# The mLSTM's maximum and weight rows: spread by matmuls with the identity instead of through DRAM

## The chip, the cores and the metric

One core of one Trainium2 chip runs the whole program. The metric is the device time of one execution in microseconds (us). Several runs are taken, and their median is given.

## The reference, cut to what matters

Two transformer blocks are computed in f32 over 1024 tokens of width 1024. The first has gated linear attention and a feed-forward part. The second has a token mixer with two halves side by side, an mLSTM with 4 heads and a latent attention with 8 heads, and then a second feed-forward part. Only the mLSTM is touched. Its recurrence over the tokens t, for each head, is

```
m_t = max(log f_t + m_{t-1}, i_t)
C_t = exp(log f_t + m_{t-1} - m_t) C_{t-1} + exp(i_t - m_t) v_t k_t^T      (n_t in the same way, with k_t alone)
h_t = C_t q_t / max(|n_t . q_t|, exp(-m_t))
```

It is computed by chunks: inside a chunk by a masked product of queries and keys, weighted by exp(D - m) with D the sums of the log gates, and across chunks by the state C. The weights need the running maximum m as a value for each query (the columns of the scores as they lie here) and for each key (the rows).

## The kernel before, in words

The kernel is one function, `tile_blocks`, with its work written out stage after stage. Matmuls of the projections take their operands split into a high and a low part and issue three products for each (L117 to L119, helper `mm3`); the mLSTM's own matmuls are plain f32.

The mLSTM works on 8 chunks of 128 tokens. A row loop (L1184 to L1203) first makes, for each chunk, four rows per head in a tile `rw` with the heads on 4 partitions: the key's value (row 0), the maximum plus the sum of gates (row 1), the exponent of the state's weight (row 2), and the key's exponent for the state (row 3). The running maximum itself is a separate tile `M_`, made by a scan on VectorE. Four transposes on TensorE (`pc`, L1202) turn the rows into columns, 16 numbers for each token, which VectorE copies to `cols`.

The chunk function `ml_chunk` needs the maximum and row 2 the other way round: the 128 queries along the free dimension and the same row on every partition. Before the change the row loop writes `M_` and row 2 to a DRAM tile `m_scr` (L1198, L1199), and each chunk reads them back with a source that repeats (L1359 for `mb`, 256 KB on arrival; two at L1363 for `wb`, 64 KB each). Then:

- ScalarE takes the exponential of `wb` (L1364). VectorE subtracts the key's column from `mb` for each of 4 heads (L1366), ScalarE takes the exponential (L1367), GpSimd applies the causal mask (L1368).
- TensorE makes the scores `msc` (L1375), VectorE multiplies them into `mb` (L1376). GpSimd scales the queries by `wb` (L1379, `mqw`). TensorE makes numerators and denominators `mnu` from `mb` (L1386) and from the state (L1388).
- TensorE transposes the keys (`mkp`, L1394), ScalarE scales them (`mkw`, L1397), TensorE makes the chunk's part of the state (`mkv`, L1402), VectorE adds it to the old state times `wb`'s last column (`mC`, L1408). The statistics `mst` and the scaled output `hn` follow (L1415 to L1428).

`mb` and `wb` have two buffers each. `msc`, `mkp` and `mkv` share two banks of PSUM (tag `y`); `mnu`, and before it `pg` and `pc`, share two (tag `tr`). Four banks (tag `big`) serve the fillers.

The fillers are projections of the attention half: 32 units with 8 matmul triples or fewer each into `pst`, then what is done with them (a norm with `cq`, a gate `to`), the transposes `pcn` of the latents and the values `pv`. Before each chunk some of them are issued (`per_chunk`), by a generator.

What each engine does in which order is fixed when the program is built: a planner goes by the order of the text and its own estimates of times, and the chunks come with a priority that is 400 instructions ahead:

```
    per_chunk = [8, 8, 6, 3, 2, 2, 2, 2]
    ...
    for t in range(NT):
        for _ in range(per_chunk[t]):
            next(units, None)
        with tc.high_priority(offset=ML_AHEAD):
            C_ = ml_chunk(t, C_)
```

All transfers are issued from SyncE's one queue, in order, and an instruction there that waits holds up those behind it.

Of the kernel before, what the change touches and what calls it, by code (L numbers as in the profile page):

```python
# [10 lines left out]
F32 = mybir.dt.float32  # L11
# [3 lines left out]
AF = mybir.ActivationFunctionType  # L15
ALU = mybir.AluOpType
# [4 lines left out]
P = 128  # L21
S = 1024
D = 1024
NT = S // P
# [15 lines left out]
def tile_blocks(ctx, tc, A, out):  # L40
    nc = tc.nc
    act, dve, pool, pe, dma = nc.scalar, nc.vector, nc.gpsimd, nc.tensor, nc.sync
# [6 lines left out]
    def nm(base):  # L49
        uid[0] += 1  # L50
        return f"{base}{uid[0]}"
# [8 lines left out]
    dram = ctx.enter_context(tc.tile_pool(name="dram", bufs=1, space=DRAM))  # L60
# [24 lines left out]
    def psum_big(n):  # L85
        return psb.tile([P, 512], F32, tag="big", name=nm(n), bufs=4)

    ident = const.tile([P, P], F32, name="ident")
# [115 lines left out]
    o_scr = dram.tile([S, 512], F32, name="o_scr")  # L204
    h_scr = dram.tile([S, 512], F32, name="h_scr")
    r_scr = dram.tile([4, 2, S], F32, name="r_scr")
    m_scr = dram.tile([4, 2, S], F32, name="m_scr")
    x1_scr = dram.tile([S, D], F32, name="x1_scr")

    f_scr = dram.tile([7, (FF // 256 - 2) * P, HALF], F32, name="f_scr")  # L210
# [64 lines left out]
    for t in range(NT):  # L275
# [9 lines left out]
        if t % 4 == 3:  # L285

            hf = t // 4
            c = slice(hf * HALF, (hf + 1) * HALF)
# [10 lines left out]
    for h0 in range(0, GH, 2):  # L299
# [3 lines left out]
        for i, (h, d) in enumerate(items):  # L303
            e, a = e4[:, i], a4[:, i]
            for hf in range(2):
                c = slice(hf * HALF, (hf + 1) * HALF)
# [6 lines left out]
        for i, (h, d) in enumerate(items):  # L313
            e, a = e4[:, i], a4[:, i]
# [204 lines left out]
    for h in range(GH):  # L519
# [3 lines left out]
        for _ in range(PANELS[h]):  # L523
            i = next(n_panels)
# [100 lines left out]
    for j in range(8):  # L625
# [5 lines left out]
        for hf in range(2):  # L631
            c = slice(hf * HALF, (hf + 1) * HALF)
# [492 lines left out]
    vpl = open_pool(ml, "vpl", side="right")  # L1125
    c2 = open_pool(ml, "c2", side="right")
    cv = ExitStack()
    cp = open_pool(cv, "cp", side="right")
# [50 lines left out]
    pool.memset(ro[:, 1, :], 0.0)  # L1179
    m0 = vpl.tile([4, 1], F32, name="m0")  # L1180
    pool.memset(m0, 0.0)
    cols = vpl.tile([P, NT, 16], F32, name="cols")
    mprev = m0
    for t in range(NT):  # L1184
        pt = ps2.tile([P, 512], F32, tag="tr", name=nm("pg"))
        pe.transpose(pt[0:4, 0:P], gts[:, t, 0:4], ident)
        pe.transpose(pt[0:4, P:2 * P], logf[:, t, :], ident)
        b_ = cp.tile([4, P], F32, tag="rb", name=nm("rb"), bufs=2)
        rw = cp.tile([4, 4, P], F32, tag="rw", name=nm("rw"), bufs=3)
        M_ = cp.tile([4, P], F32, tag="rM", name=nm("rM"), bufs=2)  # L1190
        dve.tensor_tensor_scan(out=b_, data0=ro[:, 0, :], data1=pt[0:4, P:2 * P], initial=0.0, op0=ALU.mult, op1=ALU.add)
        dve.tensor_sub(out=rw[:, 0, :], in0=pt[0:4, 0:P], in1=b_)
        dve.tensor_tensor_scan(out=M_, data0=ro[:, 1, :], data1=rw[:, 0, :], initial=mprev, op0=ALU.add, op1=ALU.max)
        dve.tensor_add(out=rw[:, 1, :], in0=b_, in1=M_)
        dve.tensor_scalar(out=rw[:, 2, :], in0=M_, scalar1=-1.0, scalar2=mprev, op0=ALU.mult, op1=ALU.add)
        dve.tensor_scalar(out=rw[:, 3, :], in0=rw[:, 0, :], scalar1=M_[:, P - 1:P], scalar2=None, op0=ALU.subtract)
        mprev = rw[:, 1, P - 1:P]
        dma.dma_start(out=m_scr[:, 0, t * P:(t + 1) * P], in_=M_)  # L1198
        dma.dma_start(out=m_scr[:, 1, t * P:(t + 1) * P], in_=rw[:, 2, :])  # L1199
        pc = ps2.tile([P, 512], F32, tag="tr", name=nm("pc"))  # L1200
        for i in range(4):
            pe.transpose(pc[:, 4 * i:4 * i + 4], rw[:, i, :], ident[0:4, 0:4])  # L1202
        dve.tensor_copy(out=cols[:, t, :], in_=pc[:, 0:16])  # L1203

    act.activation(out=cols[:, :, 4:8], in_=cols[:, :, 4:8], func=AF.Exp, scale=-1.0)
    act.activation(out=cols[:, :, 12:16], in_=cols[:, :, 12:16], func=AF.Exp)
# [148 lines left out]
    def ml_chunk(t, C_):  # L1355
        c = slice(t * P, (t + 1) * P)

        mb = mla.tile([P, 4, P], F32, tag="mb", name=nm("mb"), bufs=2)
        dma.dma_start(out=mb, in_=m_scr[:, 0, c].unsqueeze(0).broadcast_to([P, 4, P]))  # L1359
        wb = mla.tile([P, 2, P], F32, tag="wb", name=nm("wb"), bufs=2)  # L1360
        mw = m_scr.rearrange("(a b) q s -> b q a s", b=2)
        for b2 in range(2):
            dma.dma_start(out=wb[64 * b2:64 * b2 + 64], in_=mw[b2, 1, :, c].unsqueeze(0).broadcast_to([64, 2, P]))  # L1363
        act.activation(out=wb, in_=wb, func=AF.Exp)  # L1364
        for h in range(4):
            dve.tensor_scalar(out=mb[:, h, :], in0=mb[:, h, :], scalar1=cols[:, t, h:h + 1], scalar2=0.0, op0=ALU.subtract, op1=ALU.max)  # L1366
        act.activation(out=mb, in_=mb, func=AF.Exp, scale=-1.0)  # L1367
        pool.tensor_mul(out=mb, in0=mb, in1=selm.unsqueeze(1).broadcast_to([P, 4, P]))  # L1368

        mb4 = mb.rearrange("p (a b) s -> p a b s", b=2)  # L1370
        for b2 in range(2):
            sc = psum_y("msc")
            r = slice(64 * b2, 64 * b2 + 64)
            for j in range(2):
                pe.matmul(sc[:, j * P:(j + 1) * P], mk[r, j, c], mq[r, j, c], start=True, stop=True)  # L1375
            dve.tensor_mul(out=mb4[:, :, b2, :], in0=sc[:, 0:256].rearrange("p (h s) -> p h s", h=2), in1=mb4[:, :, b2, :])  # L1376
        if C_ is not None:
            qw = mlp_.tile([P, 2, P], F32, tag="qw", name=nm("mqw"), bufs=2)
            pool.tensor_mul(out=qw, in0=mq[:, :, c], in1=wb)  # L1379
        nums = []  # L1380
        for h2_ in range(2):
            nu = ps2.tile([P, 512], F32, tag="tr", name=nm("mnu"), bufs=2)
            for p2 in range(2):
                r = slice(64 * h2_, 64 * h2_ + 64)
                o = nu[:, p2 * 130:p2 * 130 + 130]
                pe.matmul(o, mb4[:, p2, h2_, :], va[t][:, 2 * p2 + h2_], start=True, stop=C_ is None)  # L1386
                if C_ is not None:
                    pe.matmul(o, qw[r, p2], C_[r, p2], start=False, stop=True)  # L1388
            nums.append(nu)

        if t < NT - 1:
            kp = psum_y("mkp")
            for p2 in range(2):
                pe.transpose(kp[:, p2 * P:(p2 + 1) * P], mk[:, p2, c], ident)  # L1394
            kw = mla.tile([P, 4, 64], F32, tag="kw", name=nm("mkw"), bufs=2)
            for h in range(4):
                act.activation(out=kw[:, h], in_=kp[:, h * 64:(h + 1) * 64], func=AF.Copy, scale=cols[:, t, 12 + h:13 + h])  # L1397
            Cn = mla.tile([P, 2, 130], F32, tag="C", name=nm("mC"), bufs=2)
            for p2 in range(2):
                kv = psum_y("mkv")  # L1400
                h0 = 2 * p2
                pe.matmul(kv[:, 0:260], kw[:, h0:h0 + 2].rearrange("p a b -> p (a b)"), va[t][:, h0:h0 + 2].rearrange("p a b -> p (a b)"), start=True, stop=True)  # L1402
                for h2_ in range(2):
                    r = slice(64 * h2_, 64 * h2_ + 64)
                    if C_ is None:
                        act.copy(out=Cn[r, p2], in_=kv[r, h2_ * 130:h2_ * 130 + 130])
                    else:
                        dve.scalar_tensor_tensor(out=Cn[r, p2], in0=C_[r, p2], scalar=wb[r, p2, P - 1:P], in1=kv[r, h2_ * 130:h2_ * 130 + 130], op0=ALU.mult, op1=ALU.add)  # L1408
            C_ = Cn

        st = mlp_.tile([P, 16], F32, tag="mst", name=nm("mst"), bufs=2)
        jk = mlp_.tile([P, P], BF16, tag="mj", name=nm("mj"), bufs=1)
        for b2 in range(2):
            n3 = nums[b2][:, 0:260].rearrange("p (h e) -> p h e", h=2)
            act.activation(out=st[:, b2:b2 + 3:2], in_=n3[:, :, 128], func=AF.Abs)  # L1415
            for a2 in range(2):
                act.activation(out=jk, in_=n3[:, a2, 0:128], func=AF.Square, accum_out=st[:, 4 + 2 * a2 + b2:5 + 2 * a2 + b2])
        dve.tensor_max(st[:, 0:4], st[:, 0:4], cols[:, t, 4:8])
        dve.reciprocal(out=st[:, 0:4], in_=st[:, 0:4])
        dve.tensor_mul(out=st[:, 8:12], in0=st[:, 0:4], in1=st[:, 0:4])  # L1420
        dve.tensor_mul(out=st[:, 8:12], in0=st[:, 8:12], in1=st[:, 4:8])
        rstd_of(st[:, 8:12], 128, 4, st[:, 12:16], st[:, 4:8])
        dve.tensor_mul(out=st[:, 8:12], in0=st[:, 12:16], in1=st[:, 0:4])
        hn = mlp_.tile([P, 512], F32, tag="hn", name=nm("hn"), bufs=1)
        for h in range(4):
            dve.scalar_tensor_tensor(out=hn[:, h * P:(h + 1) * P], in0=nums[h % 2][:, (h // 2) * 130:(h // 2) * 130 + 128],
                                     scalar=st[:, 8 + h:9 + h], in1=hnb[:, h * P:(h + 1) * P], op0=ALU.mult, op1=ALU.mult)
        dma.dma_start(out=h_scr[t * P:(t + 1) * P, :], in_=hn)  # L1428
        return C_
# [186 lines left out]
    for i in range(len(rows) + DC + 1):  # L1616
        if i < len(rows):
            h, t = rows[i]
# [11 lines left out]
        if 0 < i <= len(rows):  # L1630
            h, t = rows[i - 1]
            if h % 2 == 1 and t in ((3, 7) if h == 7 else (7,)):
                att_recip(h // 2, t - 3 if h == 7 else 0, 4 if h == 7 else 8)
        if 0 <= i - DB < len(rows):
            h, t = rows[i - DB]
# [122 lines left out]
```

## Time and profile before

| | us |
|---|---|
| runs | 2745.82, 2746.67, 2744.04; median 2745.82 |
| the profiled execution's own time | 2743.75 |
| its span in the trace | 2742.0 |
| TensorE busy (matmuls) | 2622.4 (96%) |
| VectorE busy | 1770.7 (65%) |
| ScalarE busy | 1138.5 (42%) |
| GpSimd busy | 787.5 (29%) |
| mean granted clock of TensorE | 0.979 |

In the trace PE is TensorE, PEld its loads of weights, DVE VectorE, ACT ScalarE, POOL GpSimd and SP SyncE; a "q" behind the name is that engine's sequencer or its queue of transfers. Lines are those of the kernel before. A busy TensorE is not TensorE at its peak: an instruction's length includes its time in the pipeline, so the cost of one in a row is read from the distance of the starts. The granted clock is given as a share of 2.4 GHz; 0.50 is 1.2 GHz.

### The profile page before, as it was taken

The page shows a single profiled execution, that of the slowest core. Times are in us where ns is not written, and L with a number is a line of the kernel's source. Part 1 is how long each engine was busy: PE and PEld are TensorE (multiplying, and loading weights), DVE is VectorE, ACT ScalarE, POOL GpSimd, SP SyncE. Part 2 cuts the span into 40 slices and gives each one's busy share as a digit, 9 for nine tenths or more (in the row PEclk, how much of TensorE's full clock was granted, in tenths as well). Part 3 has the DMA queues.
Part 4 walks back from the last instruction along what each step waited for, and adds up shares of the span by engine and source line. Part 5 has one row for each costly group of instructions (what it writes and reads, how often), then busy time and mean ns, then how long its engine had stood idle before and what let it go on. Part 6 is the DMA issues. An engine that isn't in the chain of part 4 may idle for free.

```text
span 2742.0 us, 36550 instructions
## 1 busy us (share of the span) xinstructions
PE 2622.4 (96%) x13651; PEld 2220.5 (81%) x13651; DVE 1770.7 (65%) x2615; ACT 1138.5 (42%) x2243; POOL 787.5 (29%) x695
## 2 busy tenths in 40 slices
PE   8989999999998999999998999999997998999998
PEld 7879898888896788887887887778895777788887
DVE  4565554474369776766777454388648766676875
ACT  4556665422124332334443432277643332354341
POOL 2333332111106544441013111123336534400014
PEclk9999999999999999999999998899998999999999
DMA  4232222453431333236441332211341433484433
GB/s 136 69 122 62 83 74 92 148 183 124 146 116 54 112 101 111 98 102 235 148 142 68 94 75 79 66 20 42 124 139 62 142 130 128 132 284 152 138 123 131
DMA packets 235889, 314.56 MB, mean 115 GB/s; under 512 B 30048, under 2 KB 157024, under 8 KB 235712
## 3 DMA queue, kind: packets, MB, share of 16 engines
q1 hardware_dynamic: 235712, 312.23, 35.1%
q8 instruction: 108, 1.77, 0.3%
q14 instruction: 69, 0.57, 0.1%
HBM read 220.36 MB, written 91.82 MB: 114 GB/s over the span
## 4 chain that ended last, share of the span: by engine, by line
PE 69%; DVE 12%; DMA 7%; issue 4%; POOL 3%; ACT 3%; SPq 1%; POOLq 0%; DVEq 0%; ACTq 0%
PE psf L119 6%; PE psf L117 6%; PE psf L118 6%; PE pw L1014 5%; PE pw L1015 5%; PE pw L1016 5%; PE pw L117 4%; PE pw L118 4%; PE pw L119 4%; DMA raw<-in_w_up_dram 3%; PE pso L118 2%; PE pso L119 2%; PE pso L117 2%; DMA mb<-m_scr 2%; DVE wo L95 1%
## 5 line engine op out<-in xcount | busy, mean ns | idle before, releaser
L117 PE MATMUL pw<-T,wo 128*128 128x512 f32 x608 | 242.8, 399 | 24.8 <-ACT wo L94 14.4
L1014 PE MATMUL pw<-op 128*128 128x512 f32 x644 | 251.6, 391 | 4.9 <-ACT a L1022 4.9
L1015 PE MATMUL pw<-op 128*128 128x512 f32 x644 | 251.8, 391 | 0.0
L1016 PE MATMUL pw<-op 128*128 128x512 f32 x644 | 251.2, 390 | 0.0
L119 PE MATMUL pw<-T,wo 128*128 128x512 f32 x608 | 238.9, 395 | 4.5 <-DVE wo L95 4.5
L118 PE MATMUL pw<-T,wo 128*128 128x512 f32 x608 | 241.0, 396 | 0.7 <-DVE T L95 0.7
L119 PE MATMUL psf<-hT,w 128*128 128x512 f32 x576 | 227.1, 394 | 0.0
L118 PE MATMUL psf<-hT,w 128*128 128x512 f32 x576 | 226.9, 394 | 0.0
L117 PE MATMUL psf<-hT,w 128*128 128x512 f32 x576 | 226.7, 393 | 0.0
L117 PE MATMUL pw<-b,wo 128*128 128x512 f32 x456 | 181.5, 398 | 18.7 <-DVE c L841 12.9
L119 PE MATMUL pw<-b,wo 128*128 128x512 f32 x456 | 179.5, 395 | 1.0 <-DVE wo L95 1.0
L118 PE MATMUL pw<-b,wo 128*128 128x512 f32 x456 | 179.6, 394 | 0.0
L94 ACT CAST op<-ar 128x1024 fp32r<-128x1024 f32 (+1 forms) x84 | 85.1, 1017 | 193.1 <-PE pw L1016 88.4
L117 PEld LDWEIGHTS pw<-T,wo 128*128 128x128 f32 x608 | 115.8, 190 | 57.8 <-ACT wo L94 15.3
L95 DVE TENSOR_TENSOR op<-ar,op 128x1024 fp32r<-128x1024 f32 (+1 forms) x84 | 100.9, 1204 | 92.4 <-ACT op L94 92.2
L95 DVE TENSOR_TENSOR w<-raw,w 128x1024 fp32r<-128x1024 f32 (+1 forms) x78 | 103.0, 1321 | 84.4 <-ACT w L94 84.1
L1014 PEld LDWEIGHTS pw<-op 128*128 128x128 f32 x644 | 121.6, 189 | 30.8 <-ACT a L1022 5.3
L95 DVE TENSOR_TENSOR wo<-s,wo 128x1024 fp32r<-128x1024 f32 x76 | 126.7, 1668 | 24.5 <-ACT wo L94 24.5
L1015 PEld LDWEIGHTS pw<-op 128*128 128x128 f32 x644 | 121.6, 189 | 25.2
L1016 PEld LDWEIGHTS pw<-op 128*128 128x128 f32 x644 | 121.5, 189 | 25.3
L119 PEld LDWEIGHTS pw<-T,wo 128*128 128x128 f32 x608 | 115.5, 190 | 31.3 <-DVE wo L95 5.9
L118 PEld LDWEIGHTS pw<-T,wo 128*128 128x128 f32 x608 | 115.7, 190 | 26.3 <-DVE T L95 2.0
(481 smaller groups left out, 7304.2 us busy)
## 6 DMA issues: line engine op xcount, KB each, us to landing
f_scr<-g SPq DMA_DIRECT2D x161, 256.0 KB
ar<-f_scr SPq DMA_DIRECT2D x69, 512.0 KB
raw<-in_w_in_dram SPq DMA_DIRECT2D x56, 512.0 KB
raw<-in_w_ffn_in_dram SPq DMA_DIRECT2D x22, 1024.0 KB
raw<-in_w_up_dram SPq DMA_DIRECT2D x16, 1024.0 KB
or<-in_w_down_dram SPq DMA_DIRECT2D x16, 1024.0 KB
or<-in_w_ffn_out_dram SPq DMA_DIRECT2D x10, 1024.0 KB
raw<-in_w_out_dram SPq DMA_DIRECT2D x16, 512.0 KB
```

The source lines that it names most:

```text
L94: act.copy(out=hl_hi, in_=src)
L95: dve.tensor_sub(out=hl_lo, in0=src, in1=hl_hi)
L117: pe.matmul(ps, ah, bh, start=(i == 0), stop=False)
L118: pe.matmul(ps, ah, bl, start=False, stop=False)
L119: pe.matmul(ps, al, bh, start=False, stop=(i == n - 1))
L1014: pe.matmul(ps, ah, bh, start=(si == 0 and k == 0), stop=False)
L1015: pe.matmul(ps, ah, bl, start=False, stop=False)
L1016: pe.matmul(ps, al, bh, start=False, stop=(end and k == q - 1))
```

## The change

The DRAM tile `m_scr` and all transfers to and from it are gone. The running maximum becomes a fifth row of `rw`, the fifth transpose of each chunk adds 4 columns to `cols` (20 instead of 16), and the copy takes all 20. In each chunk, TensorE spreads the rows: a matmul whose weights are one column of `cols` repeated over all columns, with the identity as the moving operand, gives on every output partition that column laid out as a row. Four such matmuls of 128 output partitions fill a PSUM tile `pmr` with the maxima of the 4 heads; four of 64 output partitions fill the half of a tile `pwr` with row 2, two heads above each other. VectorE's subtraction reads `pmr` and ScalarE's first exponential reads `pwr`, and both write `mb` and `wb` in SBUF as before. The two PSUM tiles are taken from the four `big` banks. The whole diff:

```diff
@@ -204,7 +204,6 @@
     o_scr = dram.tile([S, 512], F32, name="o_scr")
     h_scr = dram.tile([S, 512], F32, name="h_scr")
     r_scr = dram.tile([4, 2, S], F32, name="r_scr")
-    m_scr = dram.tile([4, 2, S], F32, name="m_scr")
     x1_scr = dram.tile([S, D], F32, name="x1_scr")
 
     f_scr = dram.tile([7, (FF // 256 - 2) * P, HALF], F32, name="f_scr")
@@ -1179,15 +1178,15 @@
     pool.memset(ro[:, 1, :], 0.0)
     m0 = vpl.tile([4, 1], F32, name="m0")
     pool.memset(m0, 0.0)
-    cols = vpl.tile([P, NT, 16], F32, name="cols")
+    cols = vpl.tile([P, NT, 20], F32, name="cols")
     mprev = m0
     for t in range(NT):
         pt = ps2.tile([P, 512], F32, tag="tr", name=nm("pg"))
         pe.transpose(pt[0:4, 0:P], gts[:, t, 0:4], ident)
         pe.transpose(pt[0:4, P:2 * P], logf[:, t, :], ident)
         b_ = cp.tile([4, P], F32, tag="rb", name=nm("rb"), bufs=2)
-        rw = cp.tile([4, 4, P], F32, tag="rw", name=nm("rw"), bufs=3)
-        M_ = cp.tile([4, P], F32, tag="rM", name=nm("rM"), bufs=2)
+        rw = cp.tile([4, 5, P], F32, tag="rw", name=nm("rw"), bufs=3)
+        M_ = rw[:, 4, :]
         dve.tensor_tensor_scan(out=b_, data0=ro[:, 0, :], data1=pt[0:4, P:2 * P], initial=0.0, op0=ALU.mult, op1=ALU.add)
         dve.tensor_sub(out=rw[:, 0, :], in0=pt[0:4, 0:P], in1=b_)
         dve.tensor_tensor_scan(out=M_, data0=ro[:, 1, :], data1=rw[:, 0, :], initial=mprev, op0=ALU.add, op1=ALU.max)
@@ -1195,12 +1194,10 @@
         dve.tensor_scalar(out=rw[:, 2, :], in0=M_, scalar1=-1.0, scalar2=mprev, op0=ALU.mult, op1=ALU.add)
         dve.tensor_scalar(out=rw[:, 3, :], in0=rw[:, 0, :], scalar1=M_[:, P - 1:P], scalar2=None, op0=ALU.subtract)
         mprev = rw[:, 1, P - 1:P]
-        dma.dma_start(out=m_scr[:, 0, t * P:(t + 1) * P], in_=M_)
-        dma.dma_start(out=m_scr[:, 1, t * P:(t + 1) * P], in_=rw[:, 2, :])
         pc = ps2.tile([P, 512], F32, tag="tr", name=nm("pc"))
-        for i in range(4):
+        for i in range(5):
             pe.transpose(pc[:, 4 * i:4 * i + 4], rw[:, i, :], ident[0:4, 0:4])
-        dve.tensor_copy(out=cols[:, t, :], in_=pc[:, 0:16])
+        dve.tensor_copy(out=cols[:, t, :], in_=pc[:, 0:20])
 
     act.activation(out=cols[:, :, 4:8], in_=cols[:, :, 4:8], func=AF.Exp, scale=-1.0)
     act.activation(out=cols[:, :, 12:16], in_=cols[:, :, 12:16], func=AF.Exp)
@@ -1356,14 +1353,18 @@
         c = slice(t * P, (t + 1) * P)
 
         mb = mla.tile([P, 4, P], F32, tag="mb", name=nm("mb"), bufs=2)
-        dma.dma_start(out=mb, in_=m_scr[:, 0, c].unsqueeze(0).broadcast_to([P, 4, P]))
+        pm = psum_big("pmr")
+        for h in range(4):
+            pe.matmul(pm[:, h * P:(h + 1) * P], cols[:, t, 16 + h:17 + h].broadcast_to([P, P]), ident, start=True, stop=True)
         wb = mla.tile([P, 2, P], F32, tag="wb", name=nm("wb"), bufs=2)
-        mw = m_scr.rearrange("(a b) q s -> b q a s", b=2)
-        for b2 in range(2):
-            dma.dma_start(out=wb[64 * b2:64 * b2 + 64], in_=mw[b2, 1, :, c].unsqueeze(0).broadcast_to([64, 2, P]))
-        act.activation(out=wb, in_=wb, func=AF.Exp)
+        pw_ = psum_big("pwr")
+        for j in range(2):
+            for e in range(2):
+                h = 2 * j + e
+                pe.matmul(pw_[64 * e:64 * e + 64, j * P:(j + 1) * P], cols[:, t, 8 + h:9 + h].broadcast_to([P, 64]), ident, start=True, stop=True)
+        act.activation(out=wb, in_=pw_[:, 0:256].rearrange("p (a s) -> p a s", a=2), func=AF.Exp)
         for h in range(4):
-            dve.tensor_scalar(out=mb[:, h, :], in0=mb[:, h, :], scalar1=cols[:, t, h:h + 1], scalar2=0.0, op0=ALU.subtract, op1=ALU.max)
+            dve.tensor_scalar(out=mb[:, h, :], in0=pm[:, h * P:(h + 1) * P], scalar1=cols[:, t, h:h + 1], scalar2=0.0, op0=ALU.subtract, op1=ALU.max)
         act.activation(out=mb, in_=mb, func=AF.Exp, scale=-1.0)
         pool.tensor_mul(out=mb, in0=mb, in1=selm.unsqueeze(1).broadcast_to([P, 4, P]))
 
```

## Rows read from the trace of the kernel before

**Rows 1.** The page: chain that ended last, share of the span by line.
```profile
PE psf L119 6%; PE psf L117 6%; PE psf L118 6%; PE pw L1014 5%; PE pw L1015 5%; PE pw L1016 5%; PE pw L117 4%; PE pw L118 4%; PE pw L119 4%; DMA raw<-in_w_up_dram 3%; PE pso L118 2%; PE pso L119 2%; PE pso L117 2%; DMA mb<-m_scr 2%; DVE wo L95 1%
```

**Rows 2.** The chain in order of time, 1100 to 1900: start us, us, what.
```profile
1677.14 7.89 DMA mb<-m_scr
```

**Rows 3.** Windows: stretch, length, busy us (instructions) of PE, PEld, DVE, ACT, POOL, PEclk, DMA.
```profile
1560.00:1612.00 52.00, 52.00 (x276) 41.59 (x275) 40.19 (x76) 18.72 (x24) 0.21 (x2) 1.00 0.24 64
...
1612.00:1785.00 173.00, 158.68 (x980) 138.36 (x978) 67.39 (x220) 51.91 (x207) 32.36 (x39) 0.88 0.29 74
...
1674.00:1752.00 78.00, 69.03 (x350) 57.57 (x351) 33.83 (x107) 22.27 (x91) 11.40 (x11) 0.76 0.28 69
1752.00:1785.00 33.00, 32.19 (x211) 27.77 (x209) 11.85 (x42) 11.19 (x46) 7.31 (x11) 1.00 0.20 63
...
1684.00:1687.00 3.00, 0.81 (x8) 0.63 (x6) 1.86 (x9) 0.96 (x3) 0.77 (x1) 1.00 0.04 9
1687.00:1690.00 3.00, 3.00 (x9) 2.11 (x10) 2.90 (x9) 0.10 (x1) 1.47 (x2) 0.53 0.11 34
```

**Rows 4.** Waits from 1610 to 1785: who for whom, total us, times, longest us.
```profile
DVE mb L1366 <- DMA mb<-m_scr: 35.0, 7, 6.2
...
PE msc L1375 <- DVE mC L1408: 9.0, 4, 4.4
...
PE pcn L1304 <- DVE cq L1142: 2.5, 1, 2.5
...
PE mnu L1386 <- DVE mb L1376: 1.4, 1, 1.4
...
SPq L1359 <- PE mnu L1386: 14.9, 6, 3.5
```

**Rows 5.** Timeline from 1674, one stall: start us, us, engine, line, [idle before].
```profile
1685.06 0.29 DVE L1366 TENSOR_SCALAR mb<-mb,cols 128x128 f32<-128x128 f32 x1 [6.09 <-DMA mb<-m_scr]
...
1686.12 1.46 DVE L1408 SCALAR_TENSOR_TENSOR mC<-mC,wb,mkv 64x130 f32<-64x130 f32 x4
...
1686.97 0.55 PE L1375 MATMUL msc<-mqk 64*128 64x128 f32 x2 [2.19 <-DVE mC L1408]
```

**Rows 6.** Timelines of TensorE from 1612 and 1674: f32 matmuls and their starts.
```profile
1614.97 0.49 PE L1375 MATMUL msc<-mqk 64*128 64x128 f32 x4
1615.39 0.39 PE L119 MATMUL pst<-w,aT 128*128 128x256 f32 x1
...
1627.81 1.16 PE L1386 MATMUL mnu<-va,mb 128*128 128x130 f32 x8 [1.40 <-DVE mb L1376]
1628.81 0.38 PE L1394 MATMUL mkp<-ident,mqk 128*128 128x128 f32 x2
...
1674.72 0.49 PE L1386 MATMUL mnu<-va,mb 128*128 128x130 f32 x2
...
1675.14 0.49 PE L1388 MATMUL mnu<-mC,mqw 64*128 64x130 f32 x2
...
1692.93 0.80 PE L1386 MATMUL mnu<-va,mb 128*128 128x130 f32 x2
...
1693.66 0.80 PE L1388 MATMUL mnu<-mC,mqw 64*128 64x130 f32 x2
```

**Rows 7.** Timeline of TensorE from 1616: `pc` among `pst`, and `pst` alone.
```profile
1616.29 0.22 PE L1202 MATMUL pc<-ident,rw 4*128 4x4 f32 x1
...
1616.76 0.22 PE L1202 MATMUL pc<-ident,rw 4*128 4x4 f32 x1
...
1617.13 0.28 PE L118 MATMUL pst<-w,aT 128*128 128x256 f32 x1
1617.25 0.28 PE L119 MATMUL pst<-w,aT 128*128 128x256 f32 x1
```

**Rows 8.** Timeline from 1674: a VectorE read of PSUM, ScalarE's exponential of `wb`.
```profile
1674.51 0.29 DVE L1306 TENSOR_TENSOR ckT<-pcn,ckT 128x128 fp32r<-128x128 f32 x1
...
1693.11 0.42 ACT L1364 ACTIVATE wb<-wb 128x256 f32<-128x256 f32 x1 [2.54 <-DMA wb<-m_scr]
```

## The prediction

> **What bounds the kernel now.** I read the page first: TensorE is busy nearly all of the span, and the chain that ended last is mostly its matmuls. Of the lines listed there one is a transfer that the kernel makes to itself, `mb<-m_scr`, at 2% [rows 1]. The chain in order of time shows what that is: single pieces of about 8 us each, such as 7.89 us from 1677.14 [rows 2]. So the change touches one stage only, and I read that stage by windows.
>
> The mLSTM chunks run from 1612 to 1785 us. There TensorE is busy 158.68 of 173.00 us, 14.3 us idle, and its mean granted clock is 0.88: 0.12 x 173 = 20.8 us of clock are lost besides [rows 3]. Most of both lies between 1674 and 1752 (69.03 of 78.00 us busy, clock 0.76). In the last 33 us, where the final chunks run and no `mb` transfer is awaited any more, TensorE is busy 32.19 us at clock 1.00. The stage before, 1560 to 1612, has no idle TensorE time (52.00 of 52.00).
>
> The waits tell why. VectorE waits 35.0 us in 7 stalls for `mb<-m_scr` at L1366 [rows 4]. The buffers of `mb` are two, so the transfer for chunk t+2 starts only when the last matmul of chunk t that reads `mb` (`mnu`) has ended; the sync queue's wait at L1359 for `mnu` says the same [rows 4]. VectorE's order has L1366 of chunk t+2 ahead of chunk t's state update L1408 (`mC`). One such stall: L1366 starts at 1685.06 after 6.09 us, L1408 follows at 1686.12, and only then can TensorE start the next scores (`msc`, 1686.97, after 2.19 us idle), because `msc` and `mkv` share two PSUM banks and L1408 frees them [rows 5]. TensorE's waits that go back to this: 9.0 us `msc` for `mC`, 2.5 us `pcn` for `cq`, 1.4 us `mnu` for `mb`, together 12.9 us [rows 4]. During the rest of each VectorE stall it lives on the filler projections (`pst`).
>
> **The change part by part.**
>
> *Removed from the stage:* per chunk three DMAs (L1359, two at L1363) and the waits of the sync queue for them; in the row loop 16 small ones (L1198, L1199). What goes is the 35.0 us of VectorE's stall, and with it the 12.9 us of TensorE's. The clock: a clock loss of 20.8 us stands for 41.5 us at half clock. A pair of f32 matmul records, `mnu` L1386 to L1388, starts 0.42 us apart at clock 1.00 and 0.73 us apart at 0.50 [rows 6], so 41.5 us of that work would take 41.5 x 0.42 / 0.73 = 23.9 us: 17.6 us to be had. The low clock follows an idle TensorE: from 1684 it is busy 0.81 us of 3 at clock 1.00, and in the next 3 us, busy throughout, the clock is 0.53 [rows 3]. The stretch almost without idle time (1752 to 1785) has 1.00, so I let the loss go with the stalls. In all 12.9 + 17.6 = 30.5 us at most. I take 28: the stretch 1752 to 1785 still has 0.8 us idle, and the first chunk's wait for the rows themselves stays.
>
> *Added on TensorE, on the path:* per chunk 4 matmuls for the maxima (`pmr`) and 4 for the weights (`pwr`), all 128 rows deep with 128 moving columns in f32. The trace shows an f32 matmul of that size as two records, so 8 x 8 x 2 = 128 records. The nearest row is `mnu<-va,mb`, 128 x 128 weights, 130 columns: 8 records from 1627.81 to the next start at 1628.81, 0.125 us each [rows 6], which gives 16.0 us. From below, `msc` (64 rows deep) takes 0.42 / 4 = 0.105 us a record (1614.97 to 1615.39): 13.4 us. From above, `mnu` alternating between 128 and 64 rows takes 0.21 us: 26.9 us; the 64-column weights of `pwr` that go to two halves of a bank might cost that. I take 16.0, because both new groups come in fours with the same depth. None of it hides: TensorE has filler to run whenever the chunk waits. This would be different only where it idles anyway.
>
> *The fifth transpose of the row loop:* 8 more of `pc`. Between two `pst` matmuls one `pc` makes the period 0.47 us (1616.29 to 1616.76), where two `pst` alone start 0.12 us apart [rows 7]: 0.35 us each, 2.8 us in a stretch where TensorE is never idle. From below, a `pc` as quick as a `pst`, 0.12 us, would make it 1.0 us. I take 2.8, since the added one joins four that are spread out in that way.
>
> *L1366 reads PSUM instead of SBUF.* From SBUF one of its pieces takes 0.29 us [rows 5]; an operation of the same 128x128 shape that reads PSUM (`ckT` L1306) takes 0.29 us too [rows 8], so I add nothing; VectorE is busy 67.39 of 173 us [rows 3]. The Trainium skill ("VectorE: DVE Perf Modes", section "Why PSUM operands drop a tier") says that an f32 operand in PSUM holds such an operation to its slowest rate, while from SBUF it may run at twice that; by the page's times for 2048 elements (1227 against 2293 ns) the estimate is 0.07 us more for each of 32. If all of that lay on the path the sum would be 2.1 us worse; by the row it is not.
>
> *The exponential of `wb` reads PSUM too*, at 0.42 us from SBUF now [rows 8]; ScalarE is busy 51.91 of 173 us [rows 3], so even a doubling (3.4 us over 8) lies beside other work. In the row loop the scan writes into `rw`, one piece of memory instead of another: nothing.
>
> *Added waits.* VectorE's L1366 and ScalarE's L1364 now wait for TensorE. Behind L1366 are queued `mst`, L1408 and `hn` of an earlier chunk, as before; but what it waits for is about a microsecond of matmul that depends on `cols` alone, which is complete when the chunks begin. What is late next is `mb`'s buffer, free with the end of `mnu`, the moment at which the transfer could only start before. The two new PSUM tiles come out of the four `big` banks that the filler uses; that is the third rival.
>
> *Sum,* against the profiled execution (2743.75 us, span 2742.0): +16.0 + 2.8 - 28 = -9.2 us, so 2734.6 us. The median of the runs shown, 2745.82, lies 2.1 us above that execution; on it I forecast 2736.6 us.
>
> **The rivals.**
>
> *Cheap matmuls.* The new records cost the lower bounds, 13.4 + 1.0, and all 30.5 us come back: -16.1 us, 2729.7 us. For it: the stretch 1752 to 1785 with its clock of 1.00. Against it: records 128 rows deep were seen at 0.125 us and the transposes at 0.35 us.
>
> *Half of it.* The order in which VectorE, ScalarE and TensorE issue is fixed ahead of time from estimates, and is laid out anew. L1366 may come to wait for a `pmr` that TensorE has behind filler, or L1408 stays late. If half of the 30.5 us returns: -15.2 + 18.8 = +3.6 us, 2749.4 us. For it: L1366 stands two chunks ahead already, with waits behind it. Against: nothing that it needs takes 8 us any more. The Trainium skill ("DMA: Bandwidth & Descriptors", the fixed and variable cost of a DMA) has about 2.0 us plus bytes over 436 GB/s, an estimate of 2.6 us for 256 KB; by it the stalls would be nearly nothing and the change would only add its 18.8 us. The chain's 7.89 us for the same transfer [rows 2] decides against it.
>
> *Slower: the PSUM banks.* `pmr` and `pwr` are ready from the start and come with a priority 400 instructions ahead, two chunks in the late part. Issued then, they hold two of the four `big` banks until `mnu` of two chunks before frees `mb` and L1408 frees `wb`; with those of a third chunk, all four. The filler has two banks or none, TensorE idles where it now runs `pst`, and the clock falls as before. If the stalls keep their 30.5 us in this form, the new work is all loss: +18.8 us, 2764.6 us. It decides once the idle time of TensorE in the stage stays above about 12 us. For it: a `cq` unit holds its bank through ScalarE, GpSimd and VectorE. Against: in the late chunks only two units of filler fall to a chunk, which one or two banks can serve.
>
> **How the numbers follow.** My forecast 0.55, cheap matmuls 0.10, half of it 0.20, the banks 0.15. A difference of 0.2% (5.5 us) is what a measurement of this kernel can tell. The forecast's own spread (records up to 0.21 us) puts some 0.08 of its share within that bound; half of it is mostly within, some on either side. Faster: 0.47 + 0.10 + 0.05 = 0.62; same: 0.08 + 0.12 + 0.02 = 0.22; slower: 0.03 + 0.13 = 0.16. The range runs from just below cheap matmuls, 2728 us, to beyond half of it, 2752 us; what lies past it is most of the banks' share.
>
> **What would show it.** Right: no wait of VectorE at L1366 over 2 us; TensorE idle under 5 us between the first and last chunk and its clock above 0.95; the new groups at 0.12 to 0.13 us a record, 16 us in all; the stage shorter by 9 us. Wrong: `pst` waiting for a `big` bank, L1366 waiting for `pmr` for microseconds, a clock below 0.9 without a DMA to blame, or a difference that arises outside the stage.

## The result, and the profile after

| kernel | median us (runs) | ratio to the runs of before beside it, 95% interval |
|---|---|---|
| before | 2746.09 (4) | |
| changed | 2764.23 (4; 2761.47 to 2767.96) | 1.0064 [1.0052, 1.0076] |

The change makes the kernel slower by 18.1 us. The forecast was 9.2 us faster, with a range up to 2752. The profiled execution of the changed kernel took 2767.96 us, 3.7 us above its median; its span is 2766.2 us.

The first `psc`, which opens the attention stage, starts at 1807.1 us instead of 1790.3: 16.8 us are lost up to there. All but 1.4 of them arise behind the first `pst` (1509.35 us against 1507.95), in the part of the kernel that the change touches. Windows of the changed kernel over that stage, columns as in [rows 3]:

```profile
1612.00:1652.00 40.00, 40.00 (x327) 38.55 (x326) 9.48 (x28) 9.61 (x28) 3.85 (x7) 1.00 0.18 55
1652.00:1690.00 38.00, 35.73 (x281) 33.04 (x280) 15.00 (x44) 14.88 (x49) 3.81 (x4) 1.00 0.35 103
1690.00:1702.00 12.00, 9.66 (x42) 7.56 (x41) 4.07 (x12) 4.58 (x19) 2.05 (x3) 0.72 0.03 12
1702.00:1756.00 54.00, 53.87 (x390) 46.60 (x390) 24.36 (x80) 19.25 (x70) 14.13 (x16) 1.00 0.10 35
1756.00:1807.00 51.00, 32.36 (x104) 22.21 (x104) 19.42 (x68) 11.23 (x52) 9.74 (x11) 0.60 0.10 29
1612.00:1807.00 195.00, 171.62 (x1136) 147.97 (x1134) 72.33 (x231) 59.54 (x217) 33.57 (x40) 0.88 0.16 49
```

The stalls every 20 us are gone: up to 1756 TensorE is busy but for some 5 us, mostly at clock 1.00. The loss has moved to the end. In the last 51 us TensorE is busy 32.36 us at a mean clock of 0.60, where the kernel before had 32.19 of its last 33.00 at 1.00 [rows 3].

The reason shows in when the fillers run. Of the changed kernel, the groups that write or read `pmr`, `pst` and `pv` (count, shortest/median/longest ns, first and last start):

```profile
L1358 PE MATMUL pmr<-ident,cols x64: 270/275/376, 1649.1 to 1750.9; 128*128 128x128 f32 x64
...
L117 PE MATMUL pst<-fw,aT x192: 279/283/581, 1628.9 to 1726.7; 128*128 128x256 f32 x192
...
L117 PE MATMUL pv<-wkv,ckT x8: 387/396/501, 1727.0 to 1748.4; 128*128 128x512 f32 x8
```

and of the kernel before:

```profile
L117 PE MATMUL pst<-fw,aT x192: 278/283/734, 1630.2 to 1778.0; 128*128 128x256 f32 x192
...
L117 PE MATMUL pv<-wkv,ckT x8: 389/395/467, 1778.3 to 1784.1; 128*128 128x512 f32 x8
```

Before, fillers ran until 1784, past the last `mnu` at 1771, and hid the end of the last chunk and the loads of the attention's first weights. Now they begin at about the same time, run undisturbed, and end at 1749; the first `pmr` starts only at 1649, and the last `mnu` at 1789. The last chunks run bare. Waits of the changed kernel from 1612 to 1807, VectorE's first, then two of TensorE's:

```profile
DVE mb L1367 <- PE pmr L1358: 22.4, 3, 12.8
...
PE pq L117 <- ACT wq L1468: 9.5, 1, 9.5
PE mnu L1387 <- DVE hn L1427: 5.7, 2, 3.8
```

VectorE's 35.0 us for the transfer [rows 4] have become 22.4 us for `pmr`, and TensorE waits 9.5 us for the attention's first weights. In the kernel before this was:

```profile
PE pq L117 <- ACT wq L1467: 0.4, 1, 0.4
```

Prices, from the changed kernel's timeline of TensorE:

```profile
1716.84 1.05 PE L1358 MATMUL pmr<-ident,cols 128*128 128x128 f32 x8
1717.82 0.66 PE L1364 MATMUL pwr<-ident,cols 128*64 128x128 f32 x8
1718.41 0.39 PE L118 MATMUL pst<-fw,aT 128*128 128x256 f32 x1
```

`pmr` takes 0.98 us for 8 records and `pwr` 0.59 us, 1.57 us a chunk and 12.6 us in all. So the work added explains less than the loss, and the stalls removed should have paid for it. Where the chunk's place comes from can be read in the order in which TensorE's instructions stand in the built program. The table counts how many of the 32 filler units have begun when chunk 0, 1, ... 7 comes to its first instruction of the kind named:

| kernel | | units begun |
|---|---|---|
| before | first `mnu` | 0, 6, 10, 12, 14, 16, 19, 22 |
| changed | `pmr` | 8, 16, 22, 25, 27, 29, 31, 32 |
| changed | first `mnu` | 10, 16, 27, 31, 32, 32, 32, 32 |

The row of `pmr` is the running sum of `per_chunk`, 8, 16, 22, 25, 27, 29, 31, 33, cut off at 32. So `pmr` of a chunk stands exactly behind all fillers that the text has ahead of it, whatever its priority. Before, even the first `mnu` of a chunk, which comes later in it, stood 8 to 13 units ahead of that.

### The profile page after: what moved, and what is told of

Its sections match the earlier page's. It is cut to its first block, busy times and chain, and to the rows that moved or that the text cites. A ratio compares the mean times of both kernels' runs of the same rounds, so it can differ in the third digit from the quotient of the medians.

```text
span 2766.2 us, 36695 instructions
## 1 busy us (share of the span) xinstructions
PE 2629.6 (95%) x13787; PEld 2226.7 (80%) x13787; DVE 1774.1 (64%) x2615; ACT 1142.8 (41%) x2243; POOL 790.3 (29%) x695
## 5 line engine op out<-in xcount | busy, mean ns | idle before, releaser
L117 PE MATMUL pw<-T,wo 128*128 128x512 f32 x608 | 242.8, 400 | 25.9 <-ACT wo L94 16.8
L117 PEld LDWEIGHTS pw<-T,wo 128*128 128x128 f32 x608 | 115.9, 191 | 58.8 <-ACT wo L94 18.1
```

What stands on the lines that cost most here:

```text
L117: pe.matmul(ps, ah, bh, start=(i == 0), stop=False)
```

## The experiments

Theory A: a tile of the tag `big` gets its bank in the order of the text. The priority does not overtake that, so a chunk that needs a `big` bank loses its head start over the fillers, and the last chunks have none left. Rival B: the added work costs what is seen, with the stalls kept in another form. Rival C, the one of the prediction: the chunks hold `big` banks and starve the fillers. Rival D: the planner ranks the new matmuls late, and a higher priority would mend it.

**ring_alone.** The kernel before, DMAs and all, tied to the `big` banks by a matmul of 4 columns.

```diff
+        pgt = psum_big("pgt")
+        pe.matmul(pgt[:, 0:4], ident, cols[:, t, 0:4], start=True, stop=True)
+        cg = mla.tile([P, 4], F32, tag="cg", name=nm("cg"), bufs=2)
+        dve.tensor_copy(out=cg, in_=pgt[:, 0:4])
...
-            dve.tensor_scalar(out=mb[:, h, :], in0=mb[:, h, :], scalar1=cols[:, t, h:h + 1], scalar2=0.0, op0=ALU.subtract, op1=ALU.max)
+            dve.tensor_scalar(out=mb[:, h, :], in0=mb[:, h, :], scalar1=cg[:, h:h + 1], scalar2=0.0, op0=ALU.subtract, op1=ALU.max)
```

> The kernel before with its DMAs kept, plus one tiny matmul per chunk that copies 4 columns of cols through a `big` bank, which L1366 then needs; 8 small matmuls in all, under 2 us of TensorE. Theory A (a tile with the tag `big` is granted its bank in the order of the text, so a chunk that needs one is tied behind the fillers written ahead of it and loses its head start; the last chunks run bare): 10 to 30 us slower than before, 2756 to 2776 us, all `pst` and `pv` done before the last two or three chunks, and there TensorE idle and its clock at 0.50. Rival B (what costs is the added TensorE work, some 12.5 us of matmuls and 2.8 us of transposes, with the stalls kept): within 2 us of before.

Measured: 2784.54 us, 1.0132 [1.0113, 1.0151], 37 us slower, more than theory A said. `pgt` stands at the same 8, 16, 22, 25, 27, 29, 31, 32 units. Its windows:

```profile
1612.00:1828.80 216.80, 172.94 (x1015) 146.66 (x1013) 71.41 (x237) 57.78 (x214) 34.16 (x41) 0.77 0.23 60
1756.00:1828.80 72.80, 42.27 (x119) 29.00 (x119) 24.32 (x82) 13.49 (x59) 12.21 (x14) 0.51 0.15 35
```

Eight small matmuls, and 73 us of bare chunks at a clock of 0.51. B falls: next to no work was added. It is dearer than the change itself. Here the bare chunks still wait for their transfers: in those 73 us VectorE waits 14.4 us for `mb<-m_scr` and TensorE 16.3 us for `mC` (9.0 us in the whole stage before [rows 4]).

**before_ahead_0.** The kernel before with its chunks not ahead of the text at all, no new tile.

```diff
-ML_AHEAD = 400
+ML_AHEAD = 0
```

> The kernel before, DMAs and all, with the chunks' priority not ahead of the text at all (0 instead of 400). No new matmul, no new PSUM tile. Theory A (what the change lost is the chunks' head start over the fillers): 2765 to 2790 us, the last chunks without filler at a TensorE clock of 0.50, as in the changed kernel. Rival B (added work): no difference over 5 us from before.

Measured: 2780.61 us, 1.0123 [1.0109, 1.0137], 35.5 us slower. The head start alone is worth what ring_alone lost.

```profile
1612.00:1826.30 214.30, 170.54 (x1011) 145.09 (x1009) 72.85 (x231) 57.92 (x216) 33.07 (x40) 0.78 0.23 62
1756.00:1826.30 70.30, 44.70 (x132) 30.77 (x132) 25.62 (x86) 14.27 (x64) 12.28 (x14) 0.52 0.15 38
```

**ahead_1200.** The changed kernel, `ML_AHEAD = 1200`.

> The changed kernel with the chunks' priority 1200 instructions ahead instead of 400. Theory A: the bank order does not go by priority, the same time within 3 us, 2761 to 2767 us, first `pmr` at 1649 us as before. Rival D (the planner put the chunks late because its estimates rank them so): first `pmr` earlier and 2735 to 2755 us.

Measured: 2762.35 us, 1.0057 [1.0039, 1.0075], and `pmr` where it was. D falls.

```profile
L1358 PE MATMUL pmr<-ident,cols x64: 270/275/376, 1648.2 to 1750.0; 128*128 128x128 f32 x64
```

**even_fill.** The changed kernel with another order of the text.

```diff
-    per_chunk = [8, 8, 6, 3, 2, 2, 2, 2]
+    per_chunk = [4, 4, 4, 4, 4, 4, 4, 4]
```

> The changed kernel with 4 filler units written ahead of each chunk instead of 8, 8, 6, 3, 2, 2, 2, 2. Theory A: filler is left for the late chunks, 2738 to 2754 us, TensorE idle under 12 us from 1612 to the first `psc`. Rival B (added work): 2760 to 2768 us.

Measured: 2753.74 us, 1.0025 [1.0015, 1.0035], 10 us less than the changed kernel and just inside theory A's range. `pmr` follows the text again, at 4, 8, 12, ... 32 units. TensorE's idle time, 20 us, was more than expected: nothing is left behind the last chunk.

```profile
1612.00:1758.00 146.00, 141.40 (x1028) 126.80 (x1027) 52.94 (x175) 48.58 (x180) 26.96 (x32) 0.98 0.18 57
1758.00:1797.90 39.90, 24.26 (x93) 17.23 (x93) 15.73 (x55) 8.36 (x36) 6.46 (x8) 0.62 0.11 30
```

**ration.** As even_fill, with `per_chunk = [2, 4, 4, 3, 3, 3, 3, 3]`; the rest follows the last chunk.

> The changed kernel, banks and priority as they are, with 2, 4, 4, 3, 3, 3, 3, 3 filler units written ahead of the chunks and 8 left behind the last. Theory A: the order of the text now leaves filler to the end: 2736 to 2750 us, faster than the even filler (2753.74 us) and than the changed kernel by 14 us or more. Rival B: 2760 to 2768 us.

Measured: 2748.58 us, 1.0012 [1.0003, 1.0020], 15.7 us less than the changed kernel; `pmr` at 2, 6, 10, 13, 16, 19, 22, 25 units. Still bare at the end: between `pmr` of the last chunk and its `mnu` the 7 units left (the expectation counted 8) run out.

```profile
1612.00:1790.70 178.70, 162.91 (x1128) 142.06 (x1128) 69.42 (x231) 57.72 (x217) 34.71 (x41) 0.94 0.17 54
1760.00:1790.70 30.70, 17.61 (x58) 12.34 (x56) 12.11 (x40) 7.95 (x28) 4.15 (x6) 0.67 0.12 31
```

**tag_y.** The changed kernel with the two tiles out of banks that no filler uses.

```diff
-        pm = psum_big("pmr")
+        pm = psum_y("pmr")
...
-        pw_ = psum_big("pwr")
+        pw_ = psum_y("pwr")
```

> The changed kernel with `pmr` and `pwr` taken from the two `y` banks, which only the chunks use. Same TensorE work. Theory A: the chunks have their head start again, 2735 to 2750 us, 14 to 29 us faster than the changed kernel; first `mnu` before 1635 us instead of 1657. Rival B (added work): 2760 to 2768 us, as the changed kernel. Rival C (the new tiles starve the fillers of `big` banks): also faster, but then the changed kernel's fillers would have to wait, while the trace after shows them early.

Measured: 2749.55 us, 1.0008 [0.9999, 1.0018], 14.7 us less than the changed kernel at the same TensorE work; the first `mnu` starts at 1626.5 us, and chunks have 0, 7, 12, 14, 16, 19, 29, 32 units begun. Up to 1766 TensorE is idle for 3 us of 154 at clock 1.00, then the end is bare:

```profile
1612.00:1766.00 154.00, 150.94 (x1091) 132.74 (x1091) 61.45 (x205) 52.21 (x198) 29.50 (x34) 1.00 0.18 56
1766.00:1791.70 25.70, 13.98 (x48) 9.58 (x45) 7.61 (x28) 4.70 (x17) 4.34 (x6) 0.60 0.14 36
```

Seven tiles a chunk now share the two `y` banks, and the last two chunks come late; that the one causes the other is not shown. But with the fillers out of their queue the priority should count again.

**tag_y_800.** tag_y with `ML_AHEAD = 800`, and **before_ahead_800**, the kernel before with the same priority.

> The changed kernel with pmr and pwr from the y banks and the priority 800 ahead. Theory A: with the banks free of fillers the priority counts again; 14 filler units are left after the last mnu, which hide the end of the last chunk and the loads of the attention's first weights. Stalls gone, 12.5 us of matmuls and some transposes paid: 2730 to 2742 us, first psc before 1785 us, TensorE clock in the stage over 0.97. Rival B (the added work eats all that the stalls give): 2745 to 2752 us.

> The kernel before with the priority 800 ahead instead of 400, as a control for tag_y_800. The 8 us transfers of mb stay and their stalls with them: 2740 to 2750 us, VectorE waiting over 25 us for mb. If a longer head start alone were the gain, it would be below 2740.

Measured: tag_y_800 2724.26 us, 0.9923 [0.9912, 0.9935], 20.8 us faster than before and better than the range given; before_ahead_800 2752.36 us, 1.0025 [1.0015, 1.0034], 2.4 us above its range. So the longer head start alone loses, and spreading by matmuls is worth 28.1 us at that priority. The chunks of tag_y_800 have 0, 2, 6, 10, 12, 14, 16, 18 units begun. Its stage:

```profile
1612.00:1771.90 159.90, 157.15 (x1112) 137.27 (x1113) 68.70 (x226) 57.04 (x215) 34.17 (x41) 1.00 0.19 61
```

Its waits of VectorE and of TensorE in that window:

```profile
DVE mb L1367 <- PE pmr L1358: 2.4, 1, 2.4
...
PE pmr L1358 <- DVE mC L1409: 1.8, 4, 0.5
```

The same of before_ahead_800:

```profile
1612.00:1795.50 183.50, 159.77 (x981) 138.22 (x980) 67.84 (x226) 54.96 (x213) 34.20 (x41) 0.89 0.27 69
```

```profile
DVE mb L1366 <- DMA mb<-m_scr: 37.6, 8, 6.6
...
PE msc L1375 <- DVE mC L1408: 12.4, 4, 4.0
```

**mb_dma** and **wb_dma.** tag_y_800 with one of the two spreads put back to DRAM. The tile `m_scr` and the write of the one row to it come back too; they are left out of the diffs below.

```diff
-        pm = psum_y("pmr")
-        for h in range(4):
-            pe.matmul(pm[:, h * P:(h + 1) * P], cols[:, t, 16 + h:17 + h].broadcast_to([P, P]), ident, start=True, stop=True)
+        dma.dma_start(out=mb, in_=m_scr[:, 0, c].unsqueeze(0).broadcast_to([P, 4, P]))
...
-            dve.tensor_scalar(out=mb[:, h, :], in0=pm[:, h * P:(h + 1) * P], scalar1=cols[:, t, h:h + 1], scalar2=0.0, op0=ALU.subtract, op1=ALU.max)
+            dve.tensor_scalar(out=mb[:, h, :], in0=mb[:, h, :], scalar1=cols[:, t, h:h + 1], scalar2=0.0, op0=ALU.subtract, op1=ALU.max)
```

```diff
-        pw_ = psum_y("pwr")
...
-        act.activation(out=wb, in_=pw_[:, 0:256].rearrange("p (a s) -> p a s", a=2), func=AF.Exp)
+        mw = m_scr.rearrange("(a b) q s -> b q a s", b=2)
+        for b2 in range(2):
+            dma.dma_start(out=wb[64 * b2:64 * b2 + 64], in_=mw[b2, 1, :, c].unsqueeze(0).broadcast_to([64, 2, P]))
+        act.activation(out=wb, in_=wb, func=AF.Exp)
```

> tag_y_800 with mb's rows read from DRAM again (one 256 KB transfer a chunk), only wb spread by matmuls. If mb's 8 us transfer is what stalls VectorE and through it TensorE: 2742 to 2754 us, near the kernel before at the same priority (2752 us), VectorE waiting over 25 us for mb. If wb's transfers are what matters: 2722 to 2730 us.

> tag_y_800 with wb read from DRAM again (two 64 KB transfers a chunk), only mb spread by matmuls; 4.7 us of TensorE work less. If mb is what matters: 2718 to 2732 us, no TensorE wait that goes back to a transfer. If wb's transfers matter as well, through ScalarE's order: 2735 to 2750 us.

Measured: mb_dma 2769.15 us, 1.0089 [1.0072, 1.0106], 15 us worse than the range; wb_dma 2735.60 us, 0.9964 [0.9951, 0.9977], just inside the case that `wb`'s transfers matter as well (2735 to 2750 us). Against tag_y_800, `mb`'s transfer put back costs 45 us, and `wb`'s two put back cost 11. The 45 us are not the price of the transfer alone, for mb_dma is 17 us slower than before_ahead_800, which has all three. In mb_dma VectorE waits for it, ScalarE's order waits behind VectorE, and TensorE waits for a `y` bank that ScalarE's exponential of `pwr` holds, a coupling that neither theory had:

```profile
DVE mb L1367 <- DMA mb<-m_scr: 41.4, 8, 6.0
ACT mb L1368 <- DVE mb L1367: 40.3, 7, 9.0
...
PE msc L1376 <- ACT wb L1365: 13.1, 4, 5.6
```

In wb_dma one stall of TensorE goes back to a transfer of `wb`, through the order of ScalarE and GpSimd. The chain in order of time (start us, us, what):

```profile
1669.77 4.76 DMA wb<-m_scr
...
1674.61 0.43 ACT wb L1365
...
1675.10 0.73 POOL mqw L1380
1675.83 1.23 POOL mb L1369
...
1677.09 0.43 DVE mb L1377
...
1677.57 0.49 PE mnu L1387 x2
```

TensorE is idle 2.0 us there, and in the 20 us around it its clock is 0.74, 5.2 us of clock:

```profile
1670.00:1690.00 20.00, 17.99 (x91) 14.99 (x90) 5.95 (x22) 4.79 (x22) 2.97 (x3) 0.74 0.20 68
```

So wb_dma shows, in this one stall, the mechanism of the second of its two cases: the exponential of `wb`, waiting for its transfer, holds up what ScalarE and GpSimd have behind it. Its last chunk besides stands at 28 units instead of 18, and the end is bare again. TensorE's waits in its stage, the longest two:

```profile
PE pq L117 <- ACT wq L1468: 7.7, 1, 7.7
PE mnu L1387 <- DVE mb L1377: 2.0, 1, 2.0
```

The second is the stall above. How much of the 11 us is the bare end and how much the transfer was not separated.

## Why the prediction was wrong

*The stalls and their cause* held. VectorE's 6 us stalls for `mb` hold up L1408 and with it TensorE and its clock: before_ahead_800 keeps them, mb_dma has them back, and in tag_y_800 idle time is 2.75 of 159.90 us at clock 1.00. The 28 us that I let come back were no exaggeration. The kernel before up to its first `psc`:

```profile
1612.00:1790.30 178.30, 163.53 (x999) 141.54 (x997) 71.65 (x228) 55.13 (x215) 33.77 (x41) 0.89 0.29 73
```

In tag_y_800 the idle time falls by 12 us against that (2.75 us, where it was 14.8), and the clock loss, 19.6 us at 0.89, by all of it.

*The size of the added work* was too high. I took 16.0 us for 128 records from `mnu`'s row [rows 6]; `pmr` has 0.1225 us a record, as read there, but `pwr` 0.074, so 12.6 us. The fear that its two halves would cost 0.21 was wrong in sign: its records start in pairs 7 ns apart, with 0.10 to 0.16 us from pair to pair, as if the two halves ran side by side. The fifth transpose was too high as well, and even the bound from below, 1.0 us. I took the price of a `pc` alone between two `pst`, but each of the 8 added ones stands right behind another `pc`. In the changed kernel:

```profile
1611.99 0.28 PE L117 MATMUL pst<-w,aT 128*128 128x256 f32 x1
1612.20 0.28 PE L1199 MATMUL pc<-ident,rw 4*128 4x4 f32 x2
1612.41 0.38 PE L118 MATMUL pst<-w,aT 128*128 128x256 f32 x1
...
1615.80 0.28 PE L118 MATMUL pst<-w,aT 128*128 128x256 f32 x1
1616.01 0.22 PE L1199 MATMUL pc<-ident,rw 4*128 4x4 f32 x1
1616.15 0.38 PE L119 MATMUL pst<-w,aT 128*128 128x256 f32 x1
```

Two `pc` put the two `pst` 0.42 us apart, one puts them 0.35 apart: 0.07 us for the second. ring_alone confirms it. From the last `pst` ahead of the row loop's transposes to the last one ahead of the fillers, TensorE does the same work there but for these 8 records and is never idle in either; it takes 77.56 us, and 78.05 in the changed kernel, 0.5 us for all 8. So the work added was 13.1 us, not 18.8.

*L1366 from PSUM* is dearer, not equal. The group before and after:

```profile
L1366 DVE TENSOR_SCALAR mb<-mb,cols x32: 278/282/289, 1622.8 to 1747.3; 128x128 f32<-128x128 f32 x32
```

```profile
L1367 DVE TENSOR_SCALAR mb<-pmr,cols x32: 339/343/352, 1650.2 to 1768.1; 128x128 f32<-128x128 f32 x32
```

That is 61 ns each. The Trainium skill ("VectorE: DVE Perf Modes", "Why PSUM operands drop a tier") gave an estimate of 70, worked out from the page's times, and the trace agrees. My row [rows 8] gave nothing: an operation with two tensor operands was no neighbour for one with a single one, and why that one is no dearer is not shown. All 32 make 2.0 us on an engine that is idle for over half of the stage; whether any of it lay on the path was not tested.

*The step that failed is the added waits.* It said that L1366 waits for a matmul "that depends on `cols` alone, which is complete when the chunks begin", and that `mb`'s buffer is late next. The matmul also depends on a bank, and the bank on every filler written before it in the text. So L1366 waits for `pmr` 22.4 us, 12.8 of them at once, which is one of the signs of being wrong that the prediction names. I had read that `big` is shared, and made a rival of it, with the direction turned round: `pmr` issued early would hold banks and starve `pst`. The fillers were never starved (TensorE busy 40.00 of 40.00 us from 1612, and no `pst` among its waits of the stage); they held up the chunks. The rival *half of it* came nearest: L1366 waiting for a `pmr` that TensorE has behind filler. But it put that down to the planner's estimates, which ahead_1200 speaks against, and priced it as half of the stalls coming back, not as the loss of the head start. The 2764.6 us of the rival of the banks is 0.4 us from the measured median by accident: it stands for lost stalls and dearer matmuls, while the runs show a loss of some 36 us for the lost head start (ring_alone, before_ahead_0) and a gain of about 18 that partly covers it (2764 against 2781 to 2785 us). The two were measured in different kernels, so their sum is an account, not a proof; tag_y_800 gives back both.

*The transfer's price* was rightly taken from the trace: at 7.9 us a transfer the stalls are real, as mb_dma shows. The Trainium skill ("DMA: Bandwidth & Descriptors", "Anatomy of one DMA — SWDGE (gpsimd) path") gives the estimate of 2.6 us in the second rival, from a fit for transfers on GpSimd's path; these are issued from SyncE, and the trace does not agree with it.

Open: tag_y_800 gains 18.4 us up to the first `psc`. The terms give 12.0 of idle time and 16.6 of clock (19.6 converted as in the prediction), less 12.6 of matmuls and 0.5 of transposes, 15.5. Of the other 2.9 us, 1.5 are there already at the first `pst` (1506.42 against 1507.95); 1.4 were not traced. Nor were the 7.4 us by which the profiled execution of the changed kernel is longer behind the first `psc`. That execution lies 3.7 us above its median and the one of before 2.3 us below, which may be most of it.

## What to carry to other kernels

A new PSUM tile has two prices: its instructions, and its place in the queue for banks. Where a stage runs ahead of other work by priority, see first whose tiles share the tag: a bank is given in the order of the text, and one tile in the common tag takes the head start of all that depends on it. When a stage is meant to be hidden, count how much filler is left behind its last step; when the last chunk comes to its first `mnu`, tag_y has none of its 32 units left and tag_y_800 has 14. The two differ in the priority alone, and by 25 us.

## What the runs showed of the hardware

- Four f32 matmuls with 64 columns of weights and 128 moving columns, written by turns to the two halves of the partitions, took 0.59 us, and four with 128 columns of weights 0.98 us, each up to the start of what follows, at clock 1.00. That is 0.074 against 0.1225 us for each of 8 records. The 64-column records start in pairs 7 ns apart, the others singly, 0.11 us apart. Whether 64 columns that all go to one half would gain the same was not run.
- A transfer that reads 2 KB of DRAM again and again to write 256 KB took 7.9 us, and two such of 64 KB a chunk held ScalarE 20 to 30 us over the 8 chunks (27.9 in the kernel before, 23.4 in wb_dma). The same two rows came from TensorE in 1.6 us a chunk.
